# A hybrid decoder trunk on one core: the state-space layer's input projection as three fp32r products ahead of the loop over units, with splits and input-matrix products on GpSimd

## The chip, the core and the metric

The kernel runs on one core of a Trainium2 chip. TensorE (PE in the profile; its weight loads are listed apart, as PEld), VectorE (DVE), ScalarE (ACT), GpSimd (POOL) and SyncE (SP) each work through a queue of their own in order, and wait for one another through semaphores. The metric is the device time of one execution in microseconds; three runs of the kernel before gave 1236.06, 1237.72 and 1237.88 us.

## The reference

One sequence of 512 tokens with 1024 channels goes through two layers. Layer 0 is a state-space (S5) mixer and a gated feed-forward block with a causal convolution, layer 1 is stick-breaking attention and another such block. Only the mixer is touched:

```python
h = rms_norm(x, norm_mix[0])
u = (h @ w_in).reshape(bsz, seq, 64, 16)                  # the input projection
# ab = exp(a*dt), bb = f * b  (complex, one 64-dim state per group of 16 channels)
bu_re = jnp.einsum('blgh,gph->blgp', u, bb_re)            # and bu_im
s[t] = ab * s[t-1] + bu[t]                                # an associative scan
y = einsum(s_re, c_re) - einsum(s_im, c_im) + d_skip * u
z = gelu(y) @ w_glu
x = x + z[..., :1024] * sigmoid(z[..., 1024:])
```

## The kernel before

The activations stay in SBUF as `x`, channels on the partitions, in 8 slices `x[:, k]` of 128 channels by 512 tokens. Outside the mixer every matrix product runs in split precision: a float32 operand is split into `hi`, its rounding to fp32r, and `lo = raw - hi`, and `gemm` issues three fp32r matmuls (hi·hi, hi·lo, lo·hi) for each slice.

In `s5` the sequence is cut into 64 chunks of 8 steps, and the 1024 channels into 8 units of 128. `u_out` (evacuation of a unit's projection with the RMS factor `rb`, to DRAM and back in another layout as `u8`), `op_b` (input-matrix products `k`, summed to `bn`), `bt_` (their transposes `bts`, two halves), `v_` (state inputs), `op_c` (output-matrix products `k`, summed to `cm`), `kk` and `kx_` (the 8-step convolution kernel, over DRAM into `m8`), `y_in`, `states` (rotate `p`, `wv`, scan `rv`, rotate back `p`, then `xv`), `y_state`, `y_turn` and `y_low` (GELU, transpose, split of the result) are each done per unit.

The projection is done here as plain float32 matmuls: unit n accumulates 8 products `u<-xg,wi` (each is recorded as two MATMUL instructions) over the gained slices `xg`, which ScalarE writes in the order of the chunks. `steps` is a generator of such filler products, first the 64 products of the projection and then the first 24 three-pass products of the output projection (`gl`), and `fill(n)` issues the next n of them. The tuple `PRE` says how many are issued at five places ahead of the loop (with 2 more behind each of three `stat` groups, which sum the squares for `rb`), and `F` how many at four places of each turn of the loop. Of the 64, 47 stand ahead of the loop, 17 in it. Four PSUM banks are shared by the 8 units, so the products of unit 4 wait until `u_out` has read unit 0's bank, and so on.

Ahead of the loop a scheduler places the instructions. In the loop over units the order on TensorE, VectorE and ScalarE is the written one (`manual_schedule`). Turn n does for unit n the input part, the states and the output; for unit n+1 `kk`, `v_`, `kx_` and the rotation tables (`turn_products`, `turn_sums`); for unit n+2 `op_b`, `bt_` and `op_c`; and it splits some of `w_glu` (`prep_hi` on ScalarE, `prep_lo` on VectorE). GpSimd does only memsets and DMA issues.

Of the kernel before, what the change touches and what calls it, by code (L numbers as in the profile page):

```python
# [17 lines left out]
P = 128  # L18
S = 512
KT = 8  # L20
# [27 lines left out]
def trunk(ctx: ExitStack, tc: tile.TileContext, A, out):  # L48
# [192 lines left out]
    def s5(st_next):  # L241
        banks_by_tag(st=1, u=2, g=2, kb=1, v=1, y=1)
        with tc.tile_pool(name="s5", bufs=1) as sp, ExitStack() as wctx:
# [21 lines left out]
            xs, sqs, bus = [], [], []  # L265

            def gained():
                k = len(xs)
                xg = T("xg", tag="ys")
                SC.activation(out=xg.rearrange("p (j c) -> p j c", j=8),  # L270
                              in_=x[:, k].rearrange("p (c j) -> p j c", j=8)[:, ::-1], func=AF.Copy,
                              scale=gcol(NMIX0, k))
                xs.append(xg)

            def square():
                k = len(sqs)
                t = T("sq", tag="ys")
                SC.activation(out=t, in_=x[:, k], func=AF.Square)
                sqs.append(t)

            for k in range(KT):
                gained()
                for _ in range(SQS[k]):
                    square()

            wis, accs = [], {}
            tags = ("u", "u", "g", "g")

            def w_load(n, q):
                raw = wp.tile([P, 8 * P], F32, tag="raw", name="wi", bufs=3)  # L290
                for c in ((slice(0, 256), slice(256, 1024)) if n == 0 else (slice(0, 1024),)):
                    q.dma_start(out=raw[:, c], in_=A["w_in"][n][:, c])
                wis.append(raw)

            w_load(0, GP)
# [6 lines left out]

            def steps():

                for n in range(KT):
                    if n > 2:
                        w_load(n, GP)
# [5 lines left out]
                    bu = B("u", tags[n % 4])  # L313
                    for k in range(KT):
                        mm(bu, wis[n][:, k * P:k * P + P], xs[k], k == 0, k == KT - 1)
                        if k == KT - 1:
                            bus.append(bu)
                        yield
                for k in range(0, KT - 2, 2):
                    while len(los) <= k // 2 or len(ys) < k + 2:  # L320
                        yield
                    for i in range(HALVES):
                        while len(u8s) < (0, 5, 6, 7)[i]:
                            yield
                        if k == 0:
                            accs[i] = B("gl", ("st", "u", "u", "g")[i])
                        for e in range(2):
                            w = [t[:, (2 * i + e) * P:(2 * i + e + 1) * P] for t in (his[k // 2], los[k // 2])]
                            gemm(accs[i], w, ys[k + e:], k1=1, first=k + e == 0, last=False)
                            yield  # L330
                while True:
                    yield
# [24 lines left out]

            def u_out(n):
                u = T("u", tag="ta")
                tt(u.rearrange("p (j c) -> p j c", j=8), bus[n].rearrange("p (j c) -> p j c", j=8),  # L360
                   rb.rearrange("p (c j) -> p j c", j=8)[:, ::-1], MUL)
# [164 lines left out]
            V.memset(tb[:, 1, :, 0:1], 0.0)  # L526
            sp2 = wctx.enter_context(tc.tile_pool(name="s5w", bufs=2))

            sh8 = [P, 4, 8, 16]

            def v5(t):
# [2 lines left out]
            def rotations():  # L534

                for lv in range(5):
                    n = 1 << lv
                    sh = [P, 2, 32, n]
                    q1, q2 = (wp.tile([P, 8 * P], F32, tag=t, name="tq")[:, :64 * n]
                              .rearrange("p (r q c) -> p r q c", r=2, q=32) for t in ("hi", "lo"))  # L540
# [46 lines left out]
            def kk(n):  # L587

                cmr, cmn = unit[n]["c"]
                bk = B("kk", "kb")  # L590
                for q in range(4):
                    o = bk[32 * q:32 * q + 32, 0:128]
                    mm(o, bdr[:, 4 * n + q], v4(cmr)[:, q], True, False)
                    mm(o, bdi[:, 4 * n + q], v4(cmn)[:, q], False, True)
                kx = sp2.tile([P, 240], F32, name="kx", bufs=1)
                GP.memset(kx[:, 0:112], 0.0)
                SC.copy(out=kx[:, 112:240], in_=bk[:, 0:128])
                unit[n]["kx"] = kx

# [14 lines left out]
            def op_b(n):  # L614

                unit[n] = {}
                k3 = products(b3, pw3, n, 1)
                yield
                bn = wide("bn", 2, "bn")
                sums(bn, k3)  # L620
                unit[n]["b"] = halves(bn)

            def bt_(n, i):
                pb = B("bt", "kb")
# [18 lines left out]
            decay = {}  # L643

            def decays(n):

                decay[n] = sp2.tile([P, 256], F32, name="mt", bufs=1)
                m4 = v4(decay[n])
                SC.copy(out=m4, in_=bc(mg8[:, 4 * n:4 * n + 4], 2, [P, 4, 64]))
                GP.memset(m4[:, :, 0:1].rearrange("p q o -> p (q o)"), 0.0)  # L650

            def states(n):

# [13 lines left out]
                rv = T("rv", tag="rv")  # L667
                for ri in range(2):
                    c = slice(256 * ri, 256 * ri + 256)
                    V.tensor_tensor_scan(out=rv[:, c], data0=decay[n], data1=wv[:, c], initial=0.0, op0=MUL, op1=ADD)  # L670
                if n + 1 < KT:
                    decays(n + 1)
                yield
# [4 lines left out]
                xv = T("xv", tag="xv")  # L678
                xv4 = xv.rearrange("p (r q c) -> p r q c", r=2, q=4)
                GP.memset(xv4[:, :, :, 0:1].rearrange("p r q o -> p (r q) o"), 0.0)  # L680
                r1 = p1.rearrange("p (r q c) -> p r q c", r=2, q=4)
                r2_ = p2.rearrange("p (r q c) -> p r q c", r=2, q=4)
                tt(xv4[:, 0, :, 1:64], r1[:, 0, :, 0:63], r2_[:, 1, :, 0:63], SUB)
# [46 lines left out]
                    if next(gen, True) is True:  # L730
                        return

            run(op_b(0))
            op_c(0)
            kk(0)
            evac()
# [5 lines left out]
            run(table, TAB0)  # L742
            evac()
            v_(0)
            run(op_b(1))
            fill(PRE[3])
            bt_(1, 0)
            bt_(1, 1)
            op_c(1)
            run(table)  # L750
            turn_products(0)
# [2 lines left out]
            fill(PRE[4])  # L754
            evac()
            decays(0)
            with tc.manual_schedule(engines={E.PE, E.DVE, E.Activation}):
                for n in range(KT):
                    more = n + 2 < KT
# [3 lines left out]
                    if n and n + 1 < KT:  # L763
                        turn_products(n + 1)
                    y_in(n)
                    st, cb = states(n), op_b(n + 2) if more else iter(())
                    for i in range(5):
                        run(st, 1)
                        run(cb, 1)
# [721 lines left out]
```

## Time and profile before

| | before |
|---|---|
| median of 3 runs | 1237.72 us |
| the profiled execution | 1236.96 us (its span: 1235.2 us) |
| granted TensorE clock, mean | 0.997 |
| first matmul | 5.80 us |
| the state matmuls of unit 0 start | 68.13 us |
| the state matmuls of unit 7 start | 149.45 us |
| TensorE busy in the span's first 160 us | 145.46 us |
| VectorE busy in the span's first 160 us | 139.79 us |
| GpSimd busy in the span's first 160 us | 19.99 us |

The page gives each engine's busy time; the rows of stretches give the same for chosen windows; the chain of waits runs back from the last instruction through whatever released it. Times of an instruction are its start and its length in us from the span's start.

### The profile page before, as it was taken

Reading aid. Unit: us, or ns where it says so; the run is one execution under the profiler, and the core shown is the slowest. Engines: PE = TensorE matmul, PEld = TensorE weight load, DVE = VectorE, ACT = ScalarE, POOL = GpSimd, SP = SyncE. Lnnn points to the kernel's source line nnn. Section 1 sums busy time; section 2 is a strip of 40 time slices with the busy share of each in tenths; the row PEclk is TensorE's granted clock in tenths of the full one; section 3 lists DMA queues with packets and bytes.
Section 4 is the critical chain, followed back from the end, with each engine's and each line's share of the span. In section 5 each row is a group of like instructions: output and inputs, shape, how many; then the busy total and the mean of one; then the engine's idle time right before and its main releaser. Section 6 shows DMA issues by size and latency. Waiting matters only on the chain.

```text
span 1235.2 us, 16227 instructions
## 1 busy us (share of the span) xinstructions
PE 1207.6 (98%) x6411; PEld 982.8 (80%) x6411; DVE 809.6 (66%) x1284; ACT 539.3 (44%) x866; POOL 24.2 (2%) x65
## 2 busy tenths in 40 slices
PE   7989999999999999999999999999999999999995
PEld 3457788788888888888889898888888888888884
DVE  7999764665435635557878989878655346536554
ACT  5234453433223323334577878765433233323331
POOL 1011020000000000000000000000000000000000
PEclk9999999999999999999999999999999999999998
DMA  5565443233233233233211211123233232332322
GB/s 199 150 166 140 122 124 98 86 102 98 90 102 99 82 106 101 92 91 100 76 51 53 82 55 48 39 86 103 86 102 97 91 103 86 91 113 88 94 75 69
DMA packets 55068, 118.47 MB, mean 96 GB/s; under 512 B 12912, under 2 KB 28528, under 8 KB 54992
## 3 DMA queue, kind: packets, MB, share of 16 engines
q1 hardware_dynamic: 50880, 105.55, 27.9%
q0 software_dynamic: 3248, 11.54, 3.1%
q8 instruction: 50, 0.82, 0.3%
q10 hardware_dynamic: 864, 0.35, 0.1%
q14 instruction: 26, 0.21, 0.1%
HBM read 109.03 MB, written 8.39 MB: 95 GB/s over the span
## 4 chain that ended last, share of the span: by engine, by line
PE 89%; DVE 8%; ACT 1%; issue 1%; DMA 1%; SPq 0%; DVEq 0%; ACTq 0%
PE fd L106 20%; PE fu L106 19%; PE fg L106 19%; PE kqb L106 7%; PE gl L106 6%; PE z L106 5%; PE ob L106 5%; PE v L106 4%; DVE k L112 2%; DVE p L112 1%; PE u L106 1%; PE y L106 1%; DVE cm L112 1%; DVE u L112 1%; DVE rv L670 1%
## 5 line engine op out<-in xcount | busy, mean ns | idle before, releaser
L106 PE MATMUL fd<-ah,wdh 128*128 128x512 f32 (+1 forms) x359 | 140.5, 391 | 0.0
L106 PE MATMUL fd<-ah,wdl 128*128 128x512 f32 (+1 forms) x359 | 139.2, 388 | 0.0
L106 PE MATMUL fd<-al,wdh 128*128 128x512 f32 (+1 forms) x359 | 137.9, 384 | 0.0
L112 DVE TENSOR_TENSOR x<-x,fd 128x512 f32<-128x512 f32 (+1 forms) x49 | 33.1, 676 | 119.8 <-PE fd L106 119.8
L157 ACT CAST wuh<-wur 128x1024 fp32r<-128x1024 f32 x44 | 46.4, 1054 | 134.4 <-PE fg L106 118.0
L157 ACT CAST wdh<-wdr 128x896 fp32r<-128x896 f32 (+1 forms) x48 | 47.1, 982 | 128.0 <-PE fd L106 98.2
L112 DVE TENSOR_TENSOR g<-fg,rb 128x512 f32<-128x512 f32 x44 | 30.4, 691 | 96.3 <-PE fg L106 93.5
L106 PE MATMUL fu<-xh,wuh 128*128 128x512 f32 x220 | 86.0, 391 | 0.0
L106 PE MATMUL fg<-xh,wgl 128*128 128x512 f32 x220 | 85.8, 390 | 0.0
L106 PE MATMUL fg<-xh,wgh 128*128 128x512 f32 x220 | 85.7, 390 | 0.0
L106 PE MATMUL fg<-xl,wgh 128*128 128x512 f32 x220 | 85.6, 389 | 0.0
L106 PE MATMUL fu<-xh,wul 128*128 128x512 f32 x220 | 85.6, 389 | 0.0
L106 PE MATMUL fu<-xl,wuh 128*128 128x512 f32 x220 | 85.6, 389 | 0.0
L112 DVE TENSOR_TENSOR u<-fu,rb 128x512 f32<-128x512 f32 x44 | 30.4, 691 | 80.5 <-PE fu L106 80.5
L106 PE MATMUL fu<-xhl,wuh 128*128 128x512 f32 x264 | 81.8, 391 | 0.0
L106 PE MATMUL fg<-xhl,wgh 128*128 128x512 f32 x264 | 81.5, 389 | 0.0
L106 PEld LDWEIGHTS fd<-ah,wdl 128*128 128x128 f32 x359 | 67.4, 188 | 15.2
L106 PEld LDWEIGHTS fd<-al,wdh 128*128 128x128 f32 x359 | 67.4, 188 | 14.8 <-issue 0.2
L106 PEld LDWEIGHTS fd<-ah,wdh 128*128 128x128 f32 x359 | 67.5, 188 | 13.2 <-issue 0.2
L157 ACT CAST wgh<-wgr 128x1024 fp32r<-128x1024 f32 x44 | 46.3, 1053 | 71.0 <-PE fd L106 33.0
L106 PE MATMUL u<-xg,wi 128*128 128x512 f32 x128 | 63.5, 628 | 7.5 <-ACT xg L270 7.5
L109 DVE SCALAR_TENSOR_TENSOR acc<-g,cw,acc 128x511 f32<-128x511 f32 x88 | 65.8, 747 | 2.4 <-ACT acc L832 0.9
(247 smaller groups left out, 2799.1 us busy)
## 6 DMA issues: line engine op xcount, KB each, us to landing
wgr<-in_w_up SPq DMA_DIRECT2D x44, 512.0 KB, 3.5
wur<-in_w_up SPq DMA_DIRECT2D x44, 512.0 KB, 3.5
wdr<-in_w_dn SPq DMA_DIRECT2D x32, 448.0 KB, 3.3
wdr<-in_w_dn SPq DMA_DIRECT2D x16, 512.0 KB, 3.5
wvr<-in_w_glu POOLq DMA_DIRECT2D x12, 512.0 KB, 3.8
ks<-kx SPq DMA_DIRECT2D x32, 128.0 KB, 2.5
m<-ks SPq DMA_DIRECT2D x8, 512.0 KB, 4.1
awr<-in_w_k SPq DMA_DIRECT2D x8, 512.0 KB, 3.5
```

The source lines that it names most:

```text
L106: PE.matmul(o, lhsT=lhsT, rhs=rhs, start=start, stop=stop, skip_group_check=True)
L109: (eng or V).scalar_tensor_tensor(out=o, in0=a, scalar=s, in1=b, op0=op0, op1=op1)
L112: (eng or V).tensor_tensor(out=o, in0=a, in1=b, op=op)
L157: SC.copy(out=hi, in_=raw)
L670: V.tensor_tensor_scan(out=rv[:, c], data0=decay[n], data1=wv[:, c], initial=0.0, op0=MUL, op1=ADD)
```

## The change

1. The projection's operands are split. For each slice, `gained` now lets ScalarE write `xg` with contiguous reads and round it to `xgh`, and GpSimd subtract to `xgl`. For each unit's weights, `w_load` lets GpSimd round (ScalarE for unit 0) to `wih` and subtract to `wil`. The 64 products are `gemm` steps of three fp32r matmuls. The reordering into chunks moves to `u_out`'s read of PSUM.
2. Units 0 and 1 are accumulated side by side, slice by slice. `PRE` now adds to 64 with the 6 behind the `stat` groups: the whole projection is issued ahead of the loop. `F` gives no filler in the first two turns and one at each of the four places in the other six.
3. `op_b` runs on GpSimd for the units numbered 2 to 7 here, in two halves over a buffer `kp`. In the loop it is issued for unit n+3, and both `bt_` stand later in the turn.
4. GpSimd's recurring memsets (zero borders of `kx`, `mt`, `xv`) are done once ahead of the loop. `rotations` uses other temporaries, and the squares for the RMS factor lie in other buffers.

```diff
-PRE = (11, 12, 10, 5, 3)
-F = ((4, 0, 3, 0), (1, 1, 1, 1), (2, 1, 1, 0), (3, 1, 1, 3), (3, 2, 1, 1), (1, 1, 1, 0), (1, 2, 2, 3), (0, 0, 3, 3))
+PRE = (11, 14, 14, 9, 10)
+F = ((0, 0, 0, 0),) * 2 + ((1, 1, 1, 1),) * 6
 def gained():
-    xg = T("xg", tag="ys")
-    SC.activation(out=xg.rearrange("p (j c) -> p j c", j=8),
-                  in_=x[:, k].rearrange("p (c j) -> p j c", j=8)[:, ::-1], func=AF.Copy,
-                  scale=gcol(NMIX0, k))
-    xs.append(xg)
+    xg, h, l = T("xg", tag="ta"), T("xgh", F32R, "ys"), T("xgl", F32R, "ys")
+    SC.activation(out=xg, in_=x[:, k], func=AF.Copy, scale=gcol(NMIX0, k))
+    SC.copy(out=h, in_=xg)
+    tt(l, xg, h, SUB, GP)
+    xs.append((h, l))
 def w_load(n, q):
     raw = wp.tile([P, 8 * P], F32, tag="raw", name="wi", bufs=3)
+    hi = wp.tile([P, 8 * P], F32R, tag="hi", name="wih")
+    lo = wp.tile([P, 8 * P], F32R, tag="lo", name="wil")
     for c in ((slice(0, 256), slice(256, 1024)) if n == 0 else (slice(0, 1024),)):
         q.dma_start(out=raw[:, c], in_=A["w_in"][n][:, c])
-    wis.append(raw)
+        if n == 0:
+            SC.copy(out=hi[:, c], in_=raw[:, c])
+        else:
+            GP.tensor_copy(out=hi[:, c], in_=raw[:, c])
+        tt(lo[:, c], raw[:, c], hi[:, c], SUB, GP)
+    wis.append((hi, lo))
 def steps():
-    mm(bu, wis[n][:, k * P:k * P + P], xs[k], k == 0, k == KT - 1)
+    for ns in ((0, 1), (2,), (3,), (4,), (5,), (6,), (7,)):
...
+        gemm(bank[n], [t[:, k * P:] for t in wis[n]], xs[k:], k1=1, first=k == 0, last=k == KT - 1)
 def op_b(n):
-    k3 = products(b3, pw3, n, 1)
-    yield
-    sums(bn, k3)
+    if n < 2:
+        sums(bn, products(b3, pw3, n, 1))
+        return
+    for i in range(2):
+        pr = slice(4 * n + 2 * i, 4 * n + 2 * i + 2)
+        kp = sp2.tile([P, 768], F32, name="kp", bufs=1)
+        tt(kp.rearrange("p (a e h) -> p a e h", a=6, e=8),
+           bc(b3[:, pr].rearrange("p a t h -> p (a t) h"), 2, [P, 6, 8, 16]),
+           bc(pw3[:, pr].rearrange("p a t e -> p (a t) e")[:, :, 1:9], 3, [P, 6, 8, 16]), MUL, GP)
...
+        tt(o4, bc(k3[:, :, 0], 1, [P, 2, 2, P]), k3[:, :, 1:3].rearrange("p a t c -> p t a c"), ADD, GP)
 # turn n of the loop
-    st, cb = states(n), op_b(n + 2) if more else iter(())
+    st = states(n)
     y8 = y_state(n)
-    if more:
-        bt_(n + 2, 0)
     fill(F[n][1])
     yy = y_turn(y8)
     if more:
-        bt_(n + 2, 1)
+        bt_(n + 2, 0)
     fill(F[n][2])
     y_low(*yy)
+    if more:
+        bt_(n + 2, 1)
+    if n + 3 < KT:
+        op_b(n + 3)
     fill(F[n][3])
```

GpSimd's queue early in the program, before the change, from the second large memset to its first two loads of weights for units 3 and 4 (`wi`):

```order
L497 MEMSET bdi 128x1024
L596 MEMSET kx 128x112
L1358 MEMSET eps 128x1
L680 MEMSET xv 128x8
L292 DMA wi<-in_w_in 128x1024
L650 MEMSET mt 128x4
```

And with the change, from the same memset on; names carry buffer numbers (`wih_165` and `wil_166` are unit 1's weights, `xgl_116` is slice 1):

```order
L510 MEMSET bdi_368 128x1024
L112 ISA
L112 TENSOR_TENSOR wil_101<-wi_99,wih_100 128x256
L112 TENSOR_TENSOR wil_101<-wi_99,wih_100 128x768
L112 TENSOR_TENSOR xgl_110<-xg_108,xgh_109 128x512
L298 CAST wih_165<-wi_164 128x1024
L112 TENSOR_TENSOR xgl_116<-xg_114,xgh_115 128x512
L112 TENSOR_TENSOR wil_166<-wi_164,wih_165 128x1024
L112 TENSOR_TENSOR xgl_122<-xg_120,xgh_121 128x512
L294 DMA wi_431<-in_w_in 128x1024
L112 TENSOR_TENSOR xgl_129<-xg_127,xgh_128 128x512
```

The splits of slices and of weights now alternate in one queue, and every slice k of the projection waits for its `xgl`.

VectorE's queue in one turn of the loop before, from the output-matrix products to the end of the states:

```order
L112 TENSOR_TENSOR k<-c_92,pwc_280 128x1536
L112 TENSOR_TENSOR cm<-k 128x1024
L112 TENSOR_TENSOR p<-v,tb 128x1024
L112 TENSOR_TENSOR k<-b_91,pw_255 128x1536
L112 TENSOR_TENSOR wv<-p 128x256 x2
L112 TENSOR_TENSOR bn<-k 128x1024
L670 SCALAR_TENSOR_TENSOR rv<-mt,wv 128x256 x2
L109 SCALAR_TENSOR_TENSOR kx<-par,kx 128x16
L112 TENSOR_TENSOR wvl<-wvr,wvh 128x1024
L112 TENSOR_TENSOR p<-rv,tb 128x1024
L112 TENSOR_TENSOR xv<-p 128x4x63
L109 SCALAR_TENSOR_TENSOR xv<-p 128x4x63
```

The same stretch with the change:

```order
L112 TENSOR_TENSOR k<-c_92,pwc_358 128x1536
L112 TENSOR_TENSOR cm<-k 128x1024
L112 TENSOR_TENSOR p<-v,tb 128x1024
L112 TENSOR_TENSOR wv<-p 128x256 x2
L691 SCALAR_TENSOR_TENSOR rv<-mt,wv 128x256 x2
L109 SCALAR_TENSOR_TENSOR kx<-par,kx 128x16
L112 TENSOR_TENSOR wvl<-wvr,wvh 128x1024
L112 TENSOR_TENSOR p<-rv,tb 128x1024
L112 TENSOR_TENSOR xv<-p 128x4x63
L109 SCALAR_TENSOR_TENSOR xv<-p 128x4x63
```

`k<-b` and `bn` are gone from the turn, and nothing stands between `wv` and the scan.

TensorE's queue in the first turn with the change, from the state matmuls of unit 0 to the `kk` of unit 2:

```order
L106 MATMUL y_860<-cm_532,xv_829 64x128 x16
L106 MATMUL yt_914<-ident_80,y8_908 64x64 x16
L651 MATMUL bt_934<-ident_80,bn_731 128x128 x4
L106 MATMUL yt_914<-yh_931,nid_89 128x512
L651 MATMUL bt_943<-ident_80,bn_731 128x128 x4
L106 MATMUL kk_957<-cm_912,bdr_367 32x128
```

Before, the first `bt` stood ahead of `yt` and the second ahead of `yt<-yh`, with `u` products between them; here both transposes come later, and no filler stands there.

More of the change, by code (lines that the diff above doesn't have):

```diff
@@ L268, in gained, with w_load @@
                 k = len(xs)
-                xg = T("xg", tag="ys")
-                SC.activation(out=xg.rearrange("p (j c) -> p j c", j=8),
-                              in_=x[:, k].rearrange("p (c j) -> p j c", j=8)[:, ::-1], func=AF.Copy,
-                              scale=gcol(NMIX0, k))
-                xs.append(xg)
+                xg, h, l = T("xg", tag="ta"), T("xgh", F32R, "ys"), T("xgl", F32R, "ys")
[3 more added lines that the diff above has]
+                xs.append((h, l))
+            sq_tiles = [T("sqb", tag="bt") for _ in range(2)] + [T("sqw", tag=t) for t in ("wv", "tq")]
+            for t in ("p", "bn"):
+                sq_tiles += halves(wide("sq2", 2, t))
             def square():
                 k = len(sqs)
-                t = T("sq", tag="ys")
+                t = sq_tiles[k]
                 SC.activation(out=t, in_=x[:, k], func=AF.Square)
                 sqs.append(t)
+            wis, accs = [], {}
+            tags = ("u", "u", "g", "g")
+            def w_load(n, q):
+                raw = wp.tile([P, 8 * P], F32, tag="raw", name="wi", bufs=3)
+                hi = wp.tile([P, 8 * P], F32R, tag="hi", name="wih")
+                lo = wp.tile([P, 8 * P], F32R, tag="lo", name="wil")
+                for c in ((slice(0, 256), slice(256, 1024)) if n == 0 else (slice(0, 1024),)):
+                    q.dma_start(out=raw[:, c], in_=A["w_in"][n][:, c])
+                    if n == 0:
[4 more added lines that the diff above has]
+                wis.append((hi, lo))
+            w_load(0, GP)
             for k in range(KT):
@@ L284, in s5 @@
                     square()
[L286 to L292, printed above, removed]
-                wis.append(raw)
-            w_load(0, GP)
             w_load(1, nc.sync)
@@ L303, in steps @@
             def steps():
-                for n in range(KT):
-                    if n > 2:
-                        w_load(n, GP)
+                for ns in ((0, 1), (2,), (3,), (4,), (5,), (6,), (7,)):
+                    for n in ns:
+                        if n > 2:
+                            w_load(n, GP)
                     if n == KT - 1:
@@ L312, in steps @@
                         yield
-                    bu = B("u", tags[n % 4])
+                    bank = {n: B("u", tags[n % 4]) for n in ns}
                     for k in range(KT):
-                        mm(bu, wis[n][:, k * P:k * P + P], xs[k], k == 0, k == KT - 1)
-                        if k == KT - 1:
-                            bus.append(bu)
-                        yield
+                        for n in ns:
+                            gemm(bank[n], [t[:, k * P:] for t in wis[n]], xs[k:], k1=1, first=k == 0, last=k == KT - 1)
+                            if k == KT - 1:
+                                bus.append(bank[n])
+                            yield
                 for k in range(0, KT - 2, 2):
@@ L359, in u_out @@
                 u = T("u", tag="ta")
-                tt(u.rearrange("p (j c) -> p j c", j=8), bus[n].rearrange("p (j c) -> p j c", j=8),
+                tt(u.rearrange("p (j c) -> p j c", j=8), bus[n].rearrange("p (c j) -> p j c", j=8)[:, ::-1],
                    rb.rearrange("p (c j) -> p j c", j=8)[:, ::-1], MUL)
@@ L527, in s5 @@
             sp2 = wctx.enter_context(tc.tile_pool(name="s5w", bufs=2))
+            zeroed = {"kx": sp2.tile([P, 240], F32, name="kx", bufs=1), "mt": sp2.tile([P, 256], F32, name="mt", bufs=1)}
+            GP.memset(zeroed["kx"][:, 0:112], 0.0)
+            GP.memset(v4(zeroed["mt"])[:, :, 0:1].rearrange("p q o -> p (q o)"), 0.0)
             sh8 = [P, 4, 8, 16]
@@ L538, in rotations @@
                     sh = [P, 2, 32, n]
-                    q1, q2 = (wp.tile([P, 8 * P], F32, tag=t, name="tq")[:, :64 * n]
-                              .rearrange("p (r q c) -> p r q c", r=2, q=32) for t in ("hi", "lo"))
+                    q1, q2 = (t[:, :64 * n].rearrange("p (r q c) -> p r q c", r=2, q=32)
+                              for t in (wide("tp", 2, "p"), TB("tp")))
                     for q_, e_ in ((q1, rot[:, 3 + lv, 0]), (q2, rot[:, 3 + lv, 1])):
@@ L594, in kk @@
                     mm(o, bdi[:, 4 * n + q], v4(cmn)[:, q], False, True)
-                kx = sp2.tile([P, 240], F32, name="kx", bufs=1)
-                GP.memset(kx[:, 0:112], 0.0)
+                kx = zeroed["kx"]
                 SC.copy(out=kx[:, 112:240], in_=bk[:, 0:128])
@@ L641, in v_ @@
                 unit[n]["v"] = vb
-            decay = {}
             def decays(n):
[L647 to L650, printed above, removed]
+                m4 = v4(zeroed["mt"])
+                SC.copy(out=m4[:, :, 1:64], in_=bc(mg8[:, 4 * n:4 * n + 4], 2, [P, 4, 63]))
             def states(n):
@@ L669, in states @@
                     c = slice(256 * ri, 256 * ri + 256)
-                    V.tensor_tensor_scan(out=rv[:, c], data0=decay[n], data1=wv[:, c], initial=0.0, op0=MUL, op1=ADD)
+                    V.tensor_tensor_scan(out=rv[:, c], data0=zeroed["mt"], data1=wv[:, c], initial=0.0, op0=MUL, op1=ADD)
                 if n + 1 < KT:
@@ L677, in states @@
                 yield
-                xv = T("xv", tag="xv")
-                xv4 = xv.rearrange("p (r q c) -> p r q c", r=2, q=4)
-                GP.memset(xv4[:, :, :, 0:1].rearrange("p r q o -> p (r q) o"), 0.0)
+                xv4 = zeroed["xv"].rearrange("p (r q c) -> p r q c", r=2, q=4)
                 r1 = p1.rearrange("p (r q c) -> p r q c", r=2, q=4)
@@ L731, in run @@
                         return
-            run(op_b(0))
+            op_b(0)
             op_c(0)
@@ L744, in s5 @@
             v_(0)
-            run(op_b(1))
+            op_b(1)
             fill(PRE[3])
@@ L748, in s5 @@
             bt_(1, 1)
+            op_b(2)
             op_c(1)
@@ L756, in s5 @@
             decays(0)
+            zeroed["xv"] = T("xv", tag="xv")
+            GP.memset(zeroed["xv"].rearrange("p (r q c) -> p r q c", r=2, q=4)[:, :, :, 0:1].rearrange("p r q o -> p (r q) o"), 0.0)
             with tc.manual_schedule(engines={E.PE, E.DVE, E.Activation}):
@@ L765, in s5 @@
                     y_in(n)
-                    st, cb = states(n), op_b(n + 2) if more else iter(())
+                    st = states(n)
                     for i in range(5):
                         run(st, 1)
-                        run(cb, 1)
                         if i == 2:
```

3 lines of the change are left out of this document (2 added, 1 removed).

## The prediction, written before the changed kernel ran

> **What bounds the kernel now.** I read the page first: busy shares and the 40 slices.
>
> ```profile
> PE 1207.6 (98%) x6411; PEld 982.8 (80%) x6411; DVE 809.6 (66%) x1284; ACT 539.3 (44%) x866; POOL 24.2 (2%) x65
> ...
> PE   7989999999999999999999999999999999999995
> ...
> DVE  7999764665435635557878989878655346536554
> ```
>
> TensorE bounds the whole, but the change touches the first five slices (31 us each), and there VectorE is as full as TensorE and TensorE is not at nine tenths everywhere. So I asked for stretches, cut where the state matmuls of a unit start (columns: stretch, length, then busy time and count of PE, PEld, DVE, ACT, POOL; clock; DMA).
>
> ```profile
> 25.00:60.00 35.00, 35.00 (x142) 16.62 (x141) 33.46 (x96) 6.24 (x19) 2.32 (x5) 1.00 0.48 135
> 60.00:68.13 8.13, 6.44 (x74) 3.65 (x73) 8.10 (x12) 1.56 (x6) 1.49 (x3) 1.00 0.55 137
> ...
> 92.59:104.89 12.30, 11.33 (x149) 7.76 (x149) 12.23 (x17) 6.24 (x16) 1.77 (x7) 1.00 0.48 129
> ...
> 139.85:149.45 9.60, 9.52 (x104) 7.54 (x103) 5.72 (x10) 2.18 (x4) 0.25 (x2) 1.00 0.48 146
> ```
>
> A turn of the loop takes 12.30 us with VectorE busy for 12.23: VectorE sets the loop. Only the last turn is TensorE's. GpSimd has almost nothing to do. From 149.45 us on TensorE runs without a gap, so what the change is worth is the shift of that moment, plus filler that is then still to do.
>
> **TensorE's own saving.** Product steps, before and in the three-pass form that the output projection already has:
>
> ```profile
> 27.39 10.55 PE L106 MATMUL u<-xg,wi 128*128 128x512 f32 x24
> ```
> ```profile
> 154.97 45.07 PE gl L106 x196
> ```
>
> A float32 product is two records at about 0.43 us, 0.86 us; three fp32r passes at 0.23 us are 0.69 us. 64 products save 64 x 0.17 = 11 us of TensorE. Little of it is on the path, since TensorE waits inside the loop anyway; what counts is when unit 0's state matmuls can start and how long a turn then takes.
>
> **Ahead of the loop, if no engine disturbs another.** Rows that set it:
>
> ```profile
> 3.80 0.47 SPq L292 DMA_DIRECT2D wi<-in_w_in  x1
> ...
> 17.47 2.17 ACT L278 ACTIVATE sq<-x 128x512 f32<-128x512 f32 x4
> ...
> 18.64 3.10 DVE L112 TENSOR_TENSOR sq<-sq 128x512 f32<-128x512 f32 x5 [2.78 <-ACT sq L278]
> ...
> 27.56 0.16 DVE L118 TENSOR_SCALAR sv<-stat 128x4 f32<-128x4 f32 x1 [1.20 <-PE stat L106]
> ```
> ```profile
> wi<-in_w_in SPq DMA_DIRECT2D x2, 512.0 KB, 10.6
> ```
> ```profile
> 36.41 0.60 DVE dg L112
> ...
> 40.70 1.00 DVE u L112
> ```
>
> ScalarE steps at 0.53 us for 128x512. Eight gains, eight squares and eight roundings (24 x 0.53 = 12.7) with the other 5 us in its queue end near 23.5 us. GpSimd is later. Unit 1's weights land at 3.80 + 10.6 = 14.4 us, and its queue holds the subtractions of slices 1 to 7 behind them.
>
> No row has GpSimd reading data. Its memset of 1024 columns repeats every 0.89 us (2.48 to 3.37, quoted below), 0.87 ns a column. One pass per operand read gives 1.74 ns for a subtraction, 0.87 for a rounding; the ends are one pass (0.87) and three (2.61, two reads and a write). I take 1.74, the middle one. So behind 14.4 us stand seven slices (7 x 0.89), two roundings (1.8), two weight subtractions (3.6), three DMA issues at 0.53 and memsets: 13.5 us, the last slice at 27.9. The third `stat` group ends near 29.4 instead of 27.5. `sv` follows at 30.5, since VectorE has some 4 us of table work moved ahead of it; from `sv` to the end of `dg` stand 10.9 us, so 41.4 against 37.0. Then `rb`, and unit 0's `u` at 43.6 to 44.6 (before 40.7 to 41.7).
>
> Unit 4's products need that bank. From there TensorE's queue has 32 steps (22.2 us), two pairs of transposes (2.4) and `v` (1.0) to the `kk` of unit 1: 70.2 us. With `kk` 0.7, its copy, `kx`, `p` and `xv`, unit 0's state matmuls start at **72.9 us**, 4.8 later than the 68.13 of before: the 17 products that stood in the loop now stand ahead of it.
>
> **A turn, if no engine disturbs another.** VectorE's chain loses `k<-b` and `bn`:
>
> ```profile
> L112 DVE TENSOR_TENSOR k<-b,pw 128x1536 f32<-128x1536 f32 x8 | 14.0, 1746 | 0.0
> ...
> L112 DVE TENSOR_TENSOR bn<-k 128x1024 f32<-128x1024 f32 x8 | 9.7, 1215 | 0.0
> ```
>
> That is about 2.8 us at issue steps, leaving 9.5. What is late next is the round through TensorE and ScalarE to `kx`, which stands ahead of `p` on VectorE:
>
> ```profile
> 92.59 1.96 PE L106 MATMUL y<-cm,xv 64*64 64x128 f32 x32 [0.81 <-DVE xv L112]
> ...
> 95.93 1.15 PE L106 MATMUL yt<-ident,y 64*64 64x64 f32 x32
> 97.01 0.66 PE L626 MATMUL bt<-ident,bn 128*128 128x128 f32 x4
> ...
> 98.69 0.45 PE L106 MATMUL kk<-cm,bdr 128*32 128x128 f32 x8
> ```
> ```profile
> 94.65 0.60 ACT L708 ACTIVATE y<-y 128x512 f32<-128x512 f32 x1 [4.13 <-PE y L106]
> ...
> 97.12 0.58 ACT L720 CAST yh<-yt 128x512 fp32r<-128x512 f32 x1 [1.31 <-PE yt L106]
> 97.76 0.58 ACT L628 COPY bts<-bt 128x512 f32<-128x512 f32 x1
> ...
> 99.28 1.05 ACT L157 CAST wvh<-wvr 128x1024 fp32r<-128x1024 f32 x1
> 100.22 0.27 ACT L597 COPY kx<-kk 128x128 f32<-128x128 f32 x1
> ```
> ```profile
> 89.71 1.14 DVE wvl L112
> 90.85 1.15 DVE p L112
> 92.02 0.42 DVE xv L112
> ```
>
> State matmuls 1.96, GELU 0.7, `yt` 1.1, `yh` 0.7, `bts` 0.6, second `bt` 0.7 (one PSUM bank, so it waits for the first copy), `bts` 0.7, `kk` 0.7, copy and `kx` 0.7, `p` 1.2, `xv` 0.4: 9.6 us. Where `wvh` and `wvl` stand in the way (three turns) it is 11.0, and the two turns with extra `u` on VectorE take 10.2 and 10.8; the last is short (7.2). The seven steps are 10.2 + 10.8 + 11.0 + 11.0 + 9.7 + 9.7 + 7.2 = 69.6 us against 149.45 - 68.13 = 81.3. TensorE has 7.2 us of unit work and 2.8 of filler per turn, under 11. Unit 7 would start at 72.9 + 69.6 = 142.5, 6.9 earlier; 3 of the 24 `gl` steps are then left over (before: none), 2.1 us. Sum without disturbance: **-4.8 us**. The other edits (fewer memsets, other temporaries) I cost at nothing: they lie on GpSimd, ScalarE or in equal VectorE work; at most 0.1 us a turn if a border's memset was waited for.
>
> **What GpSimd does to VectorE.** The one place where both work at once with large operands is the start:
>
> ```profile
> 2.48 0.97 POOL L496 MEMSET bdr<- 128x1024 f32 x1
> 2.77 1.76 DVE L118 TENSOR_SCALAR small<-par 128x32 f32<-128x32 f32 x1 [1.66 <-DMA par<-in_par]
> ...
> 3.37 0.97 POOL L497 MEMSET bdi<- 128x1024 f32 x1
> ...
> 4.40 0.15 POOL L1358 MEMSET eps<- 128x1 f32 x1
> ```
> ```profile
> L116 DVE TENSOR_SCALAR small<-small 128x32 f32<-128x32 f32 x9 | 1.5, 177 | 0.1
> ```
>
> A VectorE instruction that otherwise takes 0.177 us took 1.76 and ended (4.53) when GpSimd's back-to-back memsets did (4.55): it stood still for them, and did not get in between two. The Trainium skill, SBUF — State Buffer, section "Who interferes with whom", says that the two share a port pair, held for a whole instruction, and that a VectorE instruction with two SBUF inputs contends with a GpSimd one that reads SBUF. By that rule nearly all of VectorE's work here would block; the trace agrees for a TENSOR_SCALAR against a memset (1.76 us), and no row here shows it for two tensors.
>
> I price it as if each stood still for the other. GpSimd's work behind 14.4 us, to the loop: 7 slices 6.2, 7 weight subtractions 12.5, 7 roundings 6.2, `op_b` of one unit 4.5: 29 us. VectorE's from there to unit 0's second `p` (66.39 before): 52 less 4 idle, less 2.8 of `op_b`, plus 1 for one more `u`: 46, of which `u` and the first `p` read PSUM (7.5). One after the other that is 14.4 + 38.5 + 29 = 82, unit 0's states at 83.5: 10.6 more than above. If none of it hid in waits it would be some 22. I take **+13**, near the lower end, since VectorE also waits for TensorE there. In the loop five units have 4.5 us each on GpSimd; VectorE waits about 1.4 us for `kx`, and `p` reads PSUM for 1.1, so 2.3 are left: **+11.5**.
>
> Sum: -4.8 + 13 + 11.5 = +19.7 us on the profiled execution's 1236.96 (0.8 below the median of the runs shown): **1256.7 us**. With one pass per column GpSimd has 17.8 us ahead of the loop (14.4 + 38.5 + 17.8 = 70.7, no later than the undisturbed chain) and 2.2 us a unit in it, which hides: 1232. With three, 12 us more ahead of the loop and 11 in it: 1280. The Trainium skill, GPSIMD Engine Reference, section "3.1 Elementwise — side-by-side cycle accounting", gives 4497 ns for an add of 2048 columns, 2.2 ns a column; the sum by it would be about 1268.
>
> **Rivals.** *No blocking* (the other side): VectorE's two-operand work runs on beside GpSimd, and only the -4.8 is left: 1232.1, or 1237 at 2.61 ns a column, since slice 7 then comes 4.9 us later (7 x 0.45 and 2 x 0.89). For it: a stop is shown only against a memset. It decides at unit 0's state matmuls: with turns of 69.6 us in all the change gains if they start before 149.45 - 2.1 - 69.6 = 77.7 us. *The wait for `kx` grows*: no blocking, but the turn stays at 11.6 us, as the two late transposes and ScalarE's queue make up what VectorE lost: 72.9 + 81.3 - 149.45 + 2.1 = +6.9, 1243.8. Against it: the rows of the round sum to 9.6. *The projection is not really ahead*: the order of instructions shows all 192 passes ahead of unit 1's `kk`, so this is out.
>
> **Chances.** Under 0.2% (2.5 us) a measurement of this kernel can hardly be told from no change. Blocking 0.53 (slower 0.50, within 0.02, faster 0.01); no blocking 0.31 (faster 0.23, within 0.08); `kx` 0.11 (slower 0.08, within 0.03); others 0.05 (faster 0.03, one hundredth each for the rest). Sums: faster 0.27, within 0.14, slower 0.59. Blocking alone gives 1238 to 1280 (two operands in one pass I hold for the least likely price); to hold 8 in 10 the range must reach the undisturbed case: 1231 to 1280.
>
> **What would show it.** VectorE rows of the same shape lengthened (`k<-c` 1.75, `cm` 1.22) while GpSimd runs, and a turn above 12.3 us: blocking. Rows unchanged and turns near 10 to 11 us: no blocking. The start of unit 0's state matmuls: 72.9 undisturbed, 84 to 95 blocked. The last `xgl` at 28 us tests GpSimd's rate. I am wrong if the two engines' waits fall together, or if GpSimd starves behind VectorE rather than stopping it.

## The result, and the profile after

The changed kernel takes 1293.58 us (median of 4 runs, 1292.29 to 1295.70) against 1237.29 (4 runs, 1236.06 to 1237.88): 1.0458 times the time before, 95% interval 1.044 to 1.0476. It is **slower by 56.3 us**; 19.7 were predicted, and the range ended at 1280. The profiled run is one of 1293.99 us. One execution of an experiment below had a granted TensorE clock of 0.75 from start to end and took 1542.97 us; nothing is read from it.

Page of the kernel after: busy times, then tenths in 40 slices of 32 us.

```profile
PE 1217.6 (94%) x6475; PEld 1010.4 (78%) x6475; DVE 841.7 (65%) x1272; ACT 539.9 (42%) x876; POOL 104.4 (8%) x92
...
PE   4776789999999999999999999999999999999996
...
DVE  9996775556553554456778898886855445635555
...
POOL 7533441000000000000000000000000000000000
PEclk9688899999999999999999999999999999999998
```

The change shows in the first seven slices: TensorE is now only four to nine tenths busy there, its granted clock falls, and GpSimd has 104 us of work where it had 24. In stretches (length, then busy time and count of PE, PEld, DVE, ACT, POOL; clock; DMA):

```profile
25.00:60.00 35.00, 25.65 (x95) 20.95 (x94) 33.09 (x97) 0.00 (x0) 22.47 (x17) 0.71 0.13 37
60.00:100.00 40.00, 30.44 (x160) 22.71 (x159) 35.02 (x48) 7.24 (x22) 18.15 (x16) 0.87 0.51 144
```

VectorE is as "busy" as before (33.09 of 35 us; before, 33.46), but part of that is waiting: an instruction that is kept from running counts as busy. Its timeline beside GpSimd's shows it:

```profile
15.62 2.08 DVE L109 SCALAR_TENSOR_TENSOR small<-small 128x32 f32<-128x32 f32 x8
17.64 3.58 DVE L112 TENSOR_TENSOR small<-small 128x32 f32<-128x32 f32 x2
...
21.34 11.36 DVE L112 TENSOR_TENSOR small<-small 128x32 f32<-128x32 f32 x5
32.62 0.17 DVE L528 COPY rot<-small 128x32 f32<-128x32 f32 x1
...
48.93 0.16 DVE L118 TENSOR_SCALAR sv<-stat 128x4 f32<-128x4 f32 x1 [1.91 <-PE stat L106]
```
```profile
25.27 2.39 POOL L112 TENSOR_TENSOR wil<-wi,wih 128x1024 fp32r<-128x1024 f32 x1
27.64 1.27 POOL L112 TENSOR_TENSOR xgl<-xg,xgh 128x512 fp32r<-128x512 f32 x1
...
31.26 1.29 POOL L112 TENSOR_TENSOR xgl<-xg,xgh 128x512 fp32r<-128x512 f32 x1
```

The same five operations in the kernel before:

```profile
13.04 0.64 DVE L112 TENSOR_TENSOR small<-small 128x32 f32<-128x32 f32 x5
```

Five operations of 0.18 us took 11.36 us and ended when GpSimd's last `xgl` did, at 32.55 us; the prediction's undisturbed reckoning had this last `xgl` at 27.9. The sums of squares stand behind them in VectorE's queue, so `sv` came at 48.93 (before: 27.56), `dg` at 67.96 (36.34). The state matmuls of units 0 to 7 start at:

| kernel | unit 0 | unit 6 | unit 7 | time |
|---|---|---|---|---|
| before | 68.13 | 139.78 | 149.45 | 1236.96 |
| after | 106.03 | 195.55 | 206.26 | 1293.99 |

37.9 us are lost up to unit 0, 18.9 from there to unit 7, and 0.2 behind. In the loop, one turn of VectorE and GpSimd:

```profile
134.01 1.21 DVE L109 SCALAR_TENSOR_TENSOR kx<-par,kx 128x16 f32<-128x16 f32 x1 [7.11 <-ACT kx L613]
...
136.27 2.29 DVE L112 TENSOR_TENSOR p<-rv,tb 128x1024 f32<-128x1024 f32 x1
138.66 1.52 DVE L112 TENSOR_TENSOR xv<-p 128x252 f32<-128x252 f32 x1
```
```profile
132.33 1.28 POOL L112 TENSOR_TENSOR bn<-kp 128x512 f32<-128x512 f32 x1 [13.90 <-PE bt L651]
133.69 1.50 POOL L112 TENSOR_TENSOR kp<-b,pw 128x768 f32<-128x768 f32 x1
135.26 2.22 POOL L112 TENSOR_TENSOR bn<-kp 128x512 f32<-128x512 f32 x1
137.56 2.35 POOL L112 TENSOR_TENSOR kp<-b,pw 128x768 f32<-128x768 f32 x1
```

`op_b` waits for the one `bn` buffer, which the late second transpose frees, and so falls on `kx`, `p` and `xv`. They took 1.21, 2.29 and 1.52 us instead of 0.21, 1.22 and 0.42: 3.2 us in this turn, and as much in the two behind it, for the 2.97 that VectorE was spared. One turn earlier it fell on `wv` (1.84 instead of 0.76) and on the scan `rv` (3.58 instead of 1.27). The rows that the prediction named as the sign, `k<-c` and `cm`, kept their 1.75 and 1.22 us: none of GpSimd's reads fell beside them.

### The profile page after: what moved, and what is told of

The parts are those of the page before. It is cut to its first block, busy times and chain, and to the rows that moved or that the text cites. A ratio compares the mean times of both kernels' runs of the same rounds, so it can differ in the third digit from the quotient of the medians.

```text
span 1292.2 us, 16349 instructions
## 1 busy us (share of the span) xinstructions
PE 1217.6 (94%) x6475; PEld 1010.4 (78%) x6475; DVE 841.7 (65%) x1272; ACT 539.9 (42%) x876; POOL 104.4 (8%) x92
## 4 chain that ended last, share of the span: by engine, by line
PE 89%; DVE 8%; issue 1%; ACT 1%; DMA 1%; DVEq 0%; ACTq 0%; SPq 0%
PE fd L106 19%; PE fu L106 19%; PE fg L106 18%; PE kqb L106 7%; PE gl L106 7%; PE z L106 5%; PE ob L106 5%; PE v L106 4%; PE u L106 2%; PE y L106 2%; DVE small L112 2%; DVE p L112 1%; PE yt L106 1%; DVE small L109 1%; DMA m<-ks 1%
## 5 line engine op out<-in xcount | busy, mean ns | idle before, releaser
L106 PE MATMUL fg<-xh,wgh 128*128 128x512 f32 x220 | 85.7, 390 | 0.0
L859 ACT ACTIVATE s<-acc 128x512 f32<-128x512 f32 x44 | 27.8, 632 | 86.8 <-DVE acc L109 86.7
```

The source lines that it names most:

```text
L106: PE.matmul(o, lhsT=lhsT, rhs=rhs, start=start, stop=stop, skip_group_check=True)
L859: SC.activation(out=s, in_=acc, func=AF.Silu)
```

## Experiments

The theory: GpSimd reading two operands keeps VectorE out. Rivals: GpSimd's results are merely late; the order of the loop is at fault; TensorE's clock is. Each run below is one execution, except the last, with ten.

**Contention alone.** Idle work on GpSimd in the kernel before, that nobody reads:

```diff
+            dm = L("dm", [2 * S])
+            for _ in range(12):
+                tt(dm[:, 0:S], x[:, 6], x[:, 7], SUB, GP)
...
-                        w_load(n, GP)
+                        w_load(n, nc.sync if n < 5 else GP)
```

> The kernel before, with 12 GpSimd subtractions of two 128x512 slices of x added ahead of the loop (15 us of GpSimd work that nobody reads); weights 3 and 4 are issued by SyncE so that they don't stand behind them. Theory (GpSimd reading two operands keeps VectorE's small operations out for as long as its run lasts): small 128x32 operations of 0.18 us take 1 us and more next to the run, sv comes 8 to 14 us later than 27.56, unit 0's state matmuls start at 75 to 82 instead of 68.1, time 1244 to 1252. Rival (the changed kernel loses by waiting for GpSimd's results; the lengthened rows next to it are of no account): sv within 1.5 us of 27.56, time 1235 to 1240.

1246.33 against 1238.16; unit 0 at 77.16, 9.0 late. `sv` was only 3.6 us late; the rest fell between `sv` and `dg` (45.29). The run itself, VectorE then GpSimd:

```profile
19.14 3.10 DVE L112 TENSOR_TENSOR sq<-sq 128x512 f32<-128x512 f32 x5
...
25.52 1.31 DVE L112 TENSOR_TENSOR rot<-small 128x32 f32<-128x32 f32 x1
```
```profile
18.80 16.52 POOL L112 TENSOR_TENSOR dm<-x 128x512 f32<-128x512 f32 x7
```

While VectorE had long operations one behind the other (19.14 to 25.5) they kept their 0.60 us each, and GpSimd stood; at the short dependent ones it came in, and they took 1.3 us. Two one-operand rows of 128x4 took as long there (1.25 and 1.27).

The control has one subtraction and then only writes:

```diff
-            for _ in range(12):
-                tt(dm[:, 0:S], x[:, 6], x[:, 7], SUB, GP)
+            tt(dm[:, 0:S], x[:, 6], x[:, 7], SUB, GP)
+            for _ in range(16):
+                GP.memset(dm, 0.0)
```

> As the run with added reads, but with one subtraction and 16 memsets of 128x1024 (14 us of GpSimd work that reads nothing) in place of the 12 subtractions. If any GpSimd instruction keeps VectorE out, as the 1.76 us row beside the memsets of bdr and bdi suggests: sv 8 to 14 us late, time 1244 to 1252, as with the reads. If it is the reading of GpSimd that VectorE's two-operand instructions wait for: only one-operand rows are lengthened, sv at most 4 us late, time 1236 to 1241.

1239.49; unit 0 at 68.96, 0.8 late. Between 22.69 and 33.74 GpSimd wrote without a gap:

```profile
22.69 11.05 POOL L304 MEMSET dm<- 128x1024 f32 x11
```
```profile
23.55 0.68 DVE L112 TENSOR_TENSOR c<-c 128x512 f32<-128x512 f32 x1
...
28.74 0.98 DVE L201 CAST sf<-si 128x4 f32<-128x4 int32 x1
```

The two-operand `c` took its usual 0.68, a one-operand cast 0.98 (before: 0.16). The 1.76 us row of the prediction was of the second kind, and no measure for tensors. The Trainium skill, SBUF — State Buffer, section "Who interferes with whom", says the same: a VectorE instruction with two SBUF inputs contends with a GpSimd one that reads SBUF, not with one that only writes it. It speaks of one instruction's wait. Is that so?

```diff
-                tt(l, xg, h, SUB, GP)
+                for i in range(4):
+                    s = slice(P * i, P * i + P)
+                    tt(l[:, s], xg[:, s], h[:, s], SUB, GP)
...
```

> The changed kernel with GpSimd's subtractions of xgl and wil cut into pieces of 128 columns (0.3 to 0.4 us instead of 1.2 and 2.4 us). If VectorE waits for one GpSimd instruction at a time and gets in at the next border: the 128x32 operations beside the run take at most 0.6 us each, unit 0's state matmuls 8 us or more earlier than 106, time 1278 to 1286. If a run that always has its next instruction ready keeps VectorE out across borders: the five operations that took 11.36 us still take 8 us or more, unit 0 at 104 or later, time 1290 to 1302 (each further instruction costs GpSimd something too).

1295.92, unit 0 at 105.70. VectorE, then GpSimd:

```profile
16.81 2.04 DVE L112 TENSOR_TENSOR small<-small 128x32 f32<-128x32 f32 x5
...
22.53 0.50 DVE L494 COPY pw<-small 128x32 f32<-128x32 f32 x1
...
24.79 7.76 DVE L112 TENSOR_TENSOR small<-small 128x32 f32<-128x32 f32 x1
```
```profile
26.26 1.69 POOL L112 TENSOR_TENSOR xgl<-xg,xgh 128x128 fp32r<-128x128 f32 x4
27.92 2.52 POOL L112 TENSOR_TENSOR wil<-wi,wih 128x128 fp32r<-128x128 f32 x6
30.41 1.68 POOL L112 TENSOR_TENSOR xgl<-xg,xgh 128x128 fp32r<-128x128 f32 x4
```

Part of the small operations did get in at a border (0.5 us each), and the five that had taken 11.36 us took 2.04, where 8 or more were expected for this outcome. But one waited 7.76 us, through more than fourteen GpSimd instructions, and unit 0 came hardly earlier. Here the measurement goes beyond what the Trainium skill says there; what decides which operation gets in at a border is open.

**Undoing one part.** The splits off GpSimd:

```diff
-                tt(l, xg, h, SUB, GP)
+                tt(l, xg, h, SUB)
...
-                        GP.tensor_copy(out=hi[:, c], in_=raw[:, c])
-                    tt(lo[:, c], raw[:, c], hi[:, c], SUB, GP)
+                        SC.copy(out=hi[:, c], in_=raw[:, c])
+                    tt(lo[:, c], raw[:, c], hi[:, c], SUB)
```

> The changed kernel with the projection's splits taken from GpSimd: xgl and wil are subtracted on VectorE, wih is rounded on ScalarE; op_b stays on GpSimd. Theory (GpSimd's dense run ahead of the loop keeps VectorE's table chain out): the five 128x32 operations that took 11.36 us take about 0.6 again, sv comes near 33 us instead of 48.9, and although VectorE now carries 8 x 0.6 + 8 x 1.2 = 14.4 us of subtractions itself, unit 0's state matmuls start at 80 to 86 instead of 106. The loop keeps its stretched turns. Time 1268 to 1275. Rival (the projection's own lateness: 64 three-pass steps ahead of the loop and TensorE at a lower clock hold unit 0 back, whoever splits): unit 0 still at 98 or later, time 1286 or more.

1266.67, just below the forecast; `sv` at 31.34, unit 0 at 84.63. That is 21.4 us earlier than in the changed kernel, although VectorE has 14 us *more* to do.

`op_b` on VectorE, in the place where the change has it:

```diff
-                if n < 2:
+                if n < KT:
                     sums(bn, products(b3, pw3, n, 1))
                     return
```

> The changed kernel with op_b of units 2 to 7 back on VectorE (one product, one sum), at the place in the program where the change has it; the projection's splits stay on GpSimd. Theory (the loop's loss is op_b's four GpSimd instructions standing on kx, p and xv of VectorE): unit 0 stays near 106, no kx above 0.3 us or p above 1.3 in the loop, turns of 12 to 13 us, units 0 to 6 in 72 to 77 us instead of 89.5, time 1278 to 1283. Rival (the turns are long because the transposes and so kk and kx come late in the turn, and the filler is spread otherwise): VectorE now has 2.8 us more per turn behind the same late kx, units 0 to 6 take 88 us or more, time 1292 or more.

1290.12: neither. Units 0 to 6 took 82.4 us. No row of these turns is lengthened, but `bn` waits for its buffer in four of them (0.56 to 4.47 us):

```profile
144.87 1.23 DVE L112 TENSOR_TENSOR bn<-k 128x1024 f32<-128x1024 f32 x1 [2.08 <-PE bt L651]
```

So the place costs something as well; turn 0 alone still took 16.8 us, for a reason that comes further below. Only the place undone, `op_b` on GpSimd:

```diff
                     y8 = y_state(n)
+                    if more:
+                        bt_(n + 2, 0)
...
                     yy = y_turn(y8)
                     if more:
-                        bt_(n + 2, 0)
+                        bt_(n + 2, 1)
...
-                    if more:
-                        bt_(n + 2, 1)
```

> The changed kernel with the transposes of the input matrix (bt) back at the places that the kernel before has: the first right behind the state matmuls, the second behind yt; op_b stays on GpSimd. The added run with op_b on VectorE kept long turns, and there bn waited 2.1 us for the late transposes of the one buffer. Theory (the place: late bt delays kk and kx, and through the one bn buffer pushes op_b into kx, p and xv): units 0 to 6 in 76 to 81 us instead of 89.5, time 1280 to 1285. Rival (the lock alone: GpSimd needs its 5.6 us a unit wherever it stands, and VectorE is full everywhere): units 0 to 6 in 86 us or more, time 1290 or more.

1290.39, units 0 to 6 in 85.7 us (turn 0 in 19.4): at the rival's edge. With GpSimd there the place is worth 3 to 4 us. And in the kernel before, `op_b` alone (the GpSimd loop of the change for n > 1, and the borders zeroed once):

```diff
-                k3 = products(b3, pw3, n, 1)
-                yield
                 bn = wide("bn", 2, "bn")
-                sums(bn, k3)
...
+                    tt(o4, bc(k3[:, :, 0], 1, [P, 2, 2, P]), k3[:, :, 1:3].rearrange("p a t c -> p t a c"), ADD, GP)
```

> The kernel before with only op_b of units 2 to 7 on GpSimd (at its old place) and the borders zeroed once, so that no memset stands behind op_b; projection and transposes as before. Theory (GpSimd's 5.6 us a unit keeps VectorE out for longer than the 2.97 us that VectorE is spared): a turn 1.5 to 3 us longer, units 0 to 6 in 79 to 88 us instead of 71.7, time 1244 to 1254. Rival (op_b on GpSimd does no harm by itself, the loop of the changed kernel is long because of its transposes): turns of 10 to 11.5 us, time 1232 to 1238.

1247.77 against 1237.76; units 0 to 6 in 81.1 us. `op_b` on GpSimd loses 10 us by itself.

What is left of the change with neither on GpSimd, and the transposes and `op_b` placed as before (the edits of the splits and of `bt` from above together, one product and one sum for each unit on VectorE, and):

```diff
-                    st = states(n)
+                    st, cb = states(n), op_b(n + 2) if more else iter(())
...
+                        run(cb, 1)
...
-                        op_b(n + 3)
```

> The changed kernel with nothing on GpSimd that reads: splits on VectorE and ScalarE, op_b on VectorE and the transposes at the places of before. What is left of the change is the projection in three passes, all of it ahead of the loop. Theory (ahead of the loop VectorE is full, so its 14.4 us of subtractions move unit 0 by as much, and the loop without GpSimd is that of before): unit 0's state matmuls at 82 to 86, units 0 to 6 in 70 to 74 us, time 1250 to 1256. Rival (a loop without projection products is slower by itself, since TensorE waits and its clock falls): units 0 to 6 in 78 us or more, time 1258 or more.

1255.07 against 1237.76; unit 0 at 85.58, units 0 to 6 in 70.3 us. One after the other, the parts are 17.3 us for the projection with its splits on VectorE, 11.6 more with `op_b` on GpSimd and its order (1266.67), 26.9 more with the splits there (1293.58). They add up because each is the difference of two neighbouring runs; in another order their sizes could be others.

**Without contention.** GpSimd only writes; left out are the low parts of the projection and the input matrix of six units, and ScalarE rounds all weights:

```diff
-                tt(l, xg, h, SUB, GP)
+                GP.memset(l.bitcast(F32), 0.0)
...
-                    tt(lo[:, c], raw[:, c], hi[:, c], SUB, GP)
+                    GP.memset(lo[:, c].bitcast(F32), 0.0)
...
+                GP.memset(bn, 0.0)
```

> The changed kernel with its order and places, but GpSimd reads nothing: xgl, wil and bn of units 2 to 7 are only written (memset with 0, so the low parts of the projection and the input matrix of six units are left out), wih is rounded on ScalarE. It shows what the change would be worth without contention, which the prediction put at -4.8 us (1232.1), unit 0's state matmuls at 72.9 and units 0 to 7 in 69.6 us. If those terms were right and only the contention was sized wrong: unit 0 at 70 to 76, units 0 to 7 in 67 to 74, time 1230 to 1238. Rival (the undisturbed turn was wrong: late transposes and the low clock keep it at 11.5 us or more whatever GpSimd does): units 0 to 7 in 79 us or more, time 1240 or more.

1247.14 against 1237.41: the rival. Unit 0 at 76.12, unit 7 at 157.56, 81.4 us later. Turns 1 to 5 took 11.9, 10.8, 10.8, 10.1 and 10.1, near the forecast (10.8, 11.0, 11.0, 9.7, 9.7); turn 0 took 15.7 instead of 10.2, the last 12.1 instead of 7.2. In both TensorE waits for `m`:

```profile
83.74 1.06 DVE L112 TENSOR_TENSOR u<-u,rb 128x512 f32<-128x512 f32 x1
...
84.82 0.38 SPq L373 DMA_DIRECT2D us<-u  x1
...
85.38 0.45 SPq L622 DMA_DIRECT2D m<-ks  x1
...
89.89 1.98 PE L106 MATMUL y<-m,u 128*64 128x128 f32 x16 [5.51 <-DMA m<-ks]
```
```profile
143.08 0.23 DVE L109 SCALAR_TENSOR_TENSOR kx<-par,kx 128x16 f32<-128x16 f32 x1 [0.35 <-ACT kx L610]
...
154.76 1.29 PE L106 MATMUL y<-m,u 128*64 128x128 f32 x16 [2.01 <-DMA m<-ks]
```

In turn 0 SyncE's queue has a store of `u` ahead of `m`, and that store waits for VectorE's `u`. The changed kernel has the same: there `u` stood behind the lengthened `wv` and `rv`, and turn 0 took 19.1 us, the longest of all:

```profile
117.06 1.05 DVE L112 TENSOR_TENSOR u<-u,rb 128x512 f32<-128x512 f32 x1
...
118.14 0.38 SPq L376 DMA_DIRECT2D us<-u  x1
118.69 0.45 SPq L625 DMA_DIRECT2D m<-ks  x1
...
123.21 1.98 PE L106 MATMUL y<-m,u 128*64 128x128 f32 x16 [8.91 <-DMA m<-ks]
```

So part of the loop's loss reaches the states through a DMA queue. With units 5 to 7's `u` issued from GpSimd's queue (same parts left out):

```diff
-                nc.sync.dma_start(out=us.rearrange("j h g c -> (h g) j c"), in_=u.rearrange("p (j c) -> p j c", j=8))
+                (GP if n > 4 else nc.sync).dma_start(out=us.rearrange("j h g c -> (h g) j c"), in_=u.rearrange("p (j c) -> p j c", j=8))
...
-                nc.sync.dma_start(out=u8, in_=us.rearrange("j h g c -> (j h) (g c)"))
+                (GP if n > 4 else nc.sync).dma_start(out=u8, in_=us.rearrange("j h g c -> (j h) (g c)"))
```

> The run in which GpSimd only writes (same parts left out), with the stores and loads of u of units 5 to 7 issued from GpSimd's queue instead of SyncE's. There turn 0 took 15.7 us, and y<-m of unit 1 waited 5.5 us for m<-ks, which SyncE issued at 85.38, behind a store of u that itself waits for VectorE. Theory (SyncE's order makes turn 0 long): m<-ks issued near 80, turn 0 in 10 to 11.5 us, time 4 to 6 us below that run's 1247.1. Rival (the way of kx through memory is as long by itself, or turn 0 is bound by something else): turn 0 in 14.5 us or more, time within 1.5 us of it.

1239.33 against 1236.20; `m` issued at 78.70, turn 0 in 10.5 us. That is 7.8 us below the run above (4 to 6 were expected): unit 7 comes 6.0 earlier, and the kernel before was 1.2 us faster beside this run. The last turn stayed at 12.5.

**TensorE's clock.** In the changed kernel the passes of the projection step at 0.23 us, and behind a long wait at 0.43:

```profile
27.10 0.39 PE L106 MATMUL u<-xgh,wil 128*128 128x512 f32 x1
27.33 0.39 PE L106 MATMUL u<-xgh,wih 128*128 128x512 f32 x1
...
38.49 1.86 PE L106 MATMUL stat<-ones,sqb 128*128 128x1 f32 x8 [8.81 <-DVE sqb L112]
...
40.79 0.63 PE L106 MATMUL u<-xgl,wih 128*128 128x512 f32 x1
41.22 0.63 PE L106 MATMUL u<-xgh,wil 128*128 128x512 f32 x1
```

Does that cost time, or only fill it? Three float32 products into the free bank, ahead of the state matmuls of every unit from 1 on:

```diff
+                    if n:
+                        wb = B("warm", "kb")
+                        for _ in range(3):
+                            mm(wb, ident, x[:, 7], True, True)
                     y8 = y_state(n)
```

> The changed kernel with three float32 products that nobody reads ahead of each unit's state matmuls from unit 1 on (2.6 us of TensorE at full clock, in a wait for xv of 3.3 to 3.8 us). Theory (the low clock after a wait costs time of its own): the state matmuls take 1.96 us instead of 2.7 to 3.7, turns 1 us shorter where they were long, time 1286 to 1290. Rival (the low clock only fills time in which TensorE would wait anyway): turns as in the changed kernel, time 1292 to 1298.

1300.07: worse. At units 1 and 5 to 7 there was no wait to fill, or none long enough; and unit 0, ahead of all these products, came 2.4 us later, at 108.38, for which no run gives the reason. Unit 2 to 3 took 13.0 us instead of 15.5. So only at units 2, 3 and 4:

```diff
-                    if n:
+                    if n in (2, 3, 4):
```

> The same kernel as warm_at_waits, whose TensorE clock was 0.75 over the whole program, so that it told nothing. If the low clock after a wait costs time of its own: turns 2 to 4 together 4 to 7 us shorter than the 45.2 us from unit 2 to unit 5 of the changed kernel, time 1286 to 1290. If not: within 1.5 us of them, time 1292 to 1296.

1288.75; from unit 2 to 5 40.3 us instead of 45.2. Unit 4 in the changed kernel, then in this one:

```profile
172.50 3.38 PE L106 MATMUL y<-cm,xv 64*64 64x128 f32 x32 [3.81 <-DVE xv L112]
```
```profile
164.12 2.74 PE L106 MATMUL warm<-x,ident 128*128 128x512 f32 x6
168.76 1.96 PE L106 MATMUL y<-cm,xv 64*64 64x128 f32 x32 [1.91 <-DVE xv L112]
```

So 4.8 us of the loss are the low clock's own, at these three waits.

**The rest of the change.** The borders zeroed once, alone:

```diff
-                GP.memset(kx[:, 0:112], 0.0)
+                kx = zeroed["kx"]
...
```

> The kernel before with only the smallest part of the change: the borders of kx, mt and xv are zeroed once ahead of the loop instead of by a memset per unit. The prediction costed it at nothing, at most 0.1 us a turn: time within 1.5 us of before, ratio 0.999 to 1.001. Rival (the borders' memsets are waited for in every turn): 2 us or more faster.

Ratio 0.9995, interval 0.9985 to 1.0004: nothing, as costed. The other temporaries of `rotations` were not run alone. No run points to a version that beats the kernel before.

## Why the prediction was wrong

| us | predicted | measured |
|---|---|---|
| unit 0, undisturbed | 72.9 | 76.1 |
| units 0 to 7, undisturbed | 69.6 | 81.4 |
| contention ahead of the loop | 13 | 29.9 |
| contention in the loop | 11.5 | 18.8 |
| left over behind | 2.1 | 0.2 |

"Undisturbed" is the run in which GpSimd only writes; contention is the changed kernel less that, and so it also holds the time that GpSimd's reading itself takes before its results are there.

- **The direction and the blocking were right**: slower, and rows beside GpSimd lengthened, though not the two that were named. The rival without blocking fell. The sum went wrong at both of its parts: the gain of the undisturbed turns was not there, and the price of the contention was too small.
- **"A turn, if no engine disturbs another"** failed at both ends of the loop, not in its middle. The round through `bt`, `kk` and `kx` was summed well; what it left out is the way of `kx` on from there, through memory to `m`. In the last turn, from `kx` at 143.08 to `y<-m` at 154.76, that is 11.7 us (7.3 from the first store to the issue of the load, 4.1 for the load), so a step of 7.2 could not be had. The rows of before could have shown it: there `kx` at 137.44 and `y<-m` at 148.42 lie 11.0 us apart. In the middle turns the stores took 4.4 to 5.8 us up to the issue of the load; why the last one takes longer is open. And at turn 0 I did not look at what stands ahead of `m` in SyncE's queue, though the change puts more units' `u` there at that time. With these 11.8 us, and 3.2 at unit 0, the undisturbed change is no gain: 1247.14 was measured where 1232.1 was forecast.
- **"What GpSimd does to VectorE", ahead of the loop**, was mis-sized twice. The price: 1.74 ns a column was taken, and alone a subtraction took 1.27 us for 512 columns and 2.39 for 1024, 2.3 to 2.5; a rounding took 1.04, not 0.89. GpSimd's part is then 7 x 1.27 + 7 x 2.39 + 7 x 1.04 + 5.6 = 38.5 us instead of 29. That and the sum of the two engines' work give 93 for unit 0, and 106 was measured. The other 13 are not in a sum of the two engines' work. VectorE itself also stood idle on the way, for 10.7 us, which such a sum does not hold: 7.83 for `kx`, 1.91 for `stat` and 0.93 for `rb`. And GpSimd's second dense run, which had to wait for `pw` from the late VectorE, fell beside the chain from `sv` to `dg`: that took 19.0 us, against 9.8 in the run in which GpSimd only writes.

```profile
44.37 4.00 POOL L112 TENSOR_TENSOR kp<-b,pw 128x768 f32<-128x768 f32 x1 [11.82 <-DVE pw L112]
```
```profile
104.16 0.24 DVE L109 SCALAR_TENSOR_TENSOR kx<-par,kx 128x16 f32<-128x16 f32 x1 [7.83 <-ACT kx L613]
```

  How much of the 13 us is TensorE's low clock (0.71 from 25 to 60 us) was not tried. An estimate from the rows for the way to `sv`: twelve passes at 0.43 instead of 0.23 us, and three `stat` groups in 5.3 instead of 2.9, make close to 5 us.
- **In the loop** 2.3 us a unit was forecast, and 3.2 is what the rows of three turns show (1.0 on `kx`, 1.07 on `p`, 1.1 on `xv`). With 3.4 on `wv` and `rv` one turn earlier and about 2 in the last, that is some 15 us for five units; with the 4.8 us of low clock, which the sum did not have, 20, near the 18.8 measured. The rows don't all lie on the path, so this is an estimate.
- **TensorE's clock** was a missing step: all rows of before had 1.00, and I did not ask what waits would do to it.
- The Trainium skill, GPSIMD Engine Reference, section "3.1 Elementwise — side-by-side cycle accounting", was nearer with its 2.2 ns a column than the 1.74 taken: 2.3 to 2.5 were measured. The sum by it, about 1268, has the same gaps in the undisturbed turns and in the waits ahead of the loop.

## What to carry to other kernels

Moving two-operand work from a full VectorE to GpSimd is not a move to a free engine: what GpSimd reads, VectorE's two-operand instructions pay for, and here the short dependent ones paid most. Of GpSimd, use its writes; or place its reads where VectorE works from PSUM or waits (in the changed kernel `u` at 81.42, with one operand in PSUM, kept its 1.07 us beside a `wil` of 2.69). When a loop gets shorter on its engines, follow each value to its next user through the DMA queues as well: who stands ahead in the queue, and how long the way through memory is.

## What was not expected of the hardware

- A dense run of GpSimd instructions that read can keep VectorE out across their borders: 7.76 us for one operation of 0.18, while others got in after 0.5. It also goes the other way: seven subtractions of 1.27 us took 16.52 beside dense VectorE work. It looks as if the engine that has its next instruction ready often keeps its place; that was not tried by itself, and the operations that did get in speak against a strict rule.
- GpSimd memsets, 11 us without a gap, did not lengthen VectorE's two-operand work beside them (0.68 for 128x512), while a cast of 128x4 went from 0.16 to 0.98.
- Behind waits of 3 to 9 us TensorE's passes stepped slower (0.43 instead of 0.23 us), and that is a cost of its own: filling three waits of the loop gave back 4.8 us. The Trainium skill, TensorE: Matmul & The Clock Gate, section "Part 1: The HAM clock gate", tells of a clock that halves after an idle window of about 3.4 us; the steps of 0.43 and 0.23 us agree.
